# Cross-entropy on one core: compute pipelined over the chunk borders of the last 16384 columns, and the first prediction load on SyncE's queue

## The chip, the cores and the metric

One core of a Trainium2 chip. Its engines go by short names: PE (TensorE), DVE (VectorE), ACT (ScalarE), POOL (GpSimd) and SyncE (SP), which here only issues DMAs and waits. SBUF is the memory in which the kernel's tiles lie. In the table of DMA queues POOL's DMAs are called software_dynamic and SyncE's hardware_dynamic (the prediction's HWDGE). The metric is the device time of one execution in microseconds (us), median over runs. Times inside an execution are read from the profile and count from the start of its span. They end about 2 us below the metric.

## The reference

```python
def reference(pred, target):            # both 8192 x 8192 float32
    eps = 1e-7
    pred = np.clip(pred, eps, 1 - eps)
    return -(target * np.log(pred) + (1 - target) * np.log(1 - pred))
```

`target` is 0 or 1, so the kernel computes -ln|p + t - 1|. Two arrays are read and one is written, 268 MB each.

## The kernel before

The arrays are seen as 128 partitions x 524288 columns. Two rings in SBUF hold 32768 columns each, predictions in float32 (overwritten by the result) and targets in bfloat16 (the DMA casts: the page counts 671.10 MB on POOL's queue, which is the targets at two bytes each, where 536.87 MB are read and 268.44 MB written). The columns go through in 38 chunks: small ones at the start, thirty of 16384, small ones at the end. Every DMA is issued by POOL. A load waits for the store that frees its place in the ring (POOL did so 30 times, 1084.9 us in all).

```python
def chunk_widths(total):
    head = [4096, 4096, 8192]
    tail = [8192, 4096, 2048, 1024, 1024]
    big = 16384
    ...
def load(k):
    c, w = at(k), widths[k]
    nc.gpsimd.dma_start(out=ring_t[:, c : c + w], in_=dram(target_f, cols[k], w))
    nc.gpsimd.dma_start(out=ring_p[:, c : c + w], in_=dram(pred_f, cols[k], w))

def store(k):
    c, w = at(k), widths[k]
    nc.gpsimd.dma_start(out=dram(out_f, cols[k], w), in_=ring_p[:, c : c + w])
# [cut: front(c, w): DVE clip, DVE add of t - 1, ACT Abs, ACT Ln; back(c, w): DVE times -1]
def compute(k):                      # pieces of SUB = 2048 columns
    c, w = at(k), widths[k]
    n = max(1, w // SUB)
    s = w // n
    for i in range(n):
        front(c + i * s, s)
        if i:
            back(c + (i - 1) * s, s)
    back(c + (n - 1) * s, s)         # the chunk is flushed before the next one starts
# [cut: loop over the chunks: store what is done and in the way, load what fits, compute(k)]
```

## Time and profile before

| | before |
|---|---|
| median time, us | 1870.94 (3 runs, 1870.53 to 1871.3) |
| span of the profiled run, us | 1868.8 |
| DMA engines busy | 99.9% |
| DVE, ACT busy | 63%, 52% |

The kernel lives at the rate of its DMA engines (busy 99.9% of the span). Hold on to 16416: these are the packets of POOL's queue. Divided by 16 engines it is 1026, and 1026 is 114 DMAs times 9: in the trace 1824 of the packets have 4 bytes, so each engine has eight packets of data and one of 4 bytes for each DMA.

The end, in stretches; the last two columns are the mean busy share of the 16 DMA engines and GB/s.

```profile
core 0: us, DVE busy (x) ACT busy (x) POOL busy (x), PEclk, DMA share, GB/s
1842.00:1850.00 8.00, 4.66 (x3) 3.21 (x3) 0.96 (x1) 1.00 0.95 412
1850.00:1857.00 7.00, 3.64 (x4) 3.20 (x3) 0.53 (x1) 1.00 0.97 417
1857.00:1861.00 4.00, 1.94 (x3) 1.97 (x2) 0.53 (x1) 1.00 0.57 237
1861.00:1865.00 4.00, 0.69 (x1) 0.15 (x1) 0.25 (x1) 1.00 0.09 38
1865.00:1868.00 3.00, 0.00 (x0) 0.00 (x0) 0.29 (x1) 1.00 0.43 175
```

And POOL's issues of the last four stores, from the timeline (start, duration, and in brackets the idle time before and what ended it).

```profile
1844.03 0.96 POOL L79 DMA_DIRECT2D out_dram<-ring_p  x1 [11.39 <-DVE ring_p L94]
1852.64 0.53 POOL L79 DMA_DIRECT2D out_dram<-ring_p  x1 [7.65 <-DVE ring_p L94]
1857.40 0.53 POOL L79 DMA_DIRECT2D out_dram<-ring_p  x1 [4.23 <-DVE ring_p L94]
1864.75 0.54 POOL L79 DMA_DIRECT2D out_dram<-ring_p  x1 [6.82 <-issue]
```

From 1857 us on the DMA engines run out of work (share 0.57, then 0.09). A share of 0.06 is one engine of 16. The last store carries a mark: its wait ended in "issue", that is, in nothing that the profile shows. DVE's last negation ended at 1861.87 us. The other three went out 0.3 us after their negations, this one 2.88 us after.

One more reading, used all through. A DMA's completion semaphore is counted up sixteen times (1824 counts for 114 DMAs, as many as there are packets of 4 bytes), which is read here as once by each of the 16 DMA engines, and the trace has the times. The sixteenth count is the landing; the distance from a middle count to the last is the lag of the slowest engine. For the store of the last 16384-column chunk but one, the first count came at 1782.19, a middle one at 1782.73, the last at 1788.55 us: the slowest engine is 5.8 us behind.

### The profile page before, as it was taken

To read this page: it belongs to the slowest core of one execution; us is meant where nothing else is said; L and a number is where in the kernel's file an instruction comes from. 1 tells how busy PE (TensorE), PEld (TensorE's weight loads), DVE (VectorE), ACT (ScalarE), POOL (GpSimd) and SP (SyncE) were. 2 spreads that over 40 slices of the span, in tenths; PEclk is the share of its full clock that TensorE was granted. 3 is DMA by queue.
4 is the path that set the end of the run, shared out by engine and by line. 5 is a ranking of instruction groups with operands and counts; after the bars stand their busy time and mean duration, and the time that the engine had idled before them with its cause. 6 is when DMAs were issued, how large, how long until landed. Compare 5 with 4: busy or idle time off the path is not lost.

```text
span 1868.8 us, 1563 instructions
## 1 busy us (share of the span) xinstructions
DVE 1178.6 (63%) x772; ACT 976.3 (52%) x516; POOL 65.4 (3%) x118
## 2 busy tenths in 40 slices
DVE  4557755577555775557755577555776556755595
ACT  3446544565444654446544466444664446644474
POOL 1000000000000000000000000000000000000010
DMA  9999999999999999999999999999999999999998
GB/s 292 359 358 338 348 400 371 337 355 342 393 386 339 341 352 387 384 351 339 345 386 389 351 344 337 383 395 344 352 344 365 400 358 339 354 355 395 374 335 349
DMA packets 16427, 671.19 MB, mean 359 GB/s; under 512 B 1824, under 2 KB 1824, under 8 KB 2720
## 3 DMA queue, kind: packets, MB, share of 16 engines
q0 software_dynamic: 16416, 671.10, 99.9%
q14 instruction: 11, 0.09, 0.0%
HBM read 536.87 MB, written 268.44 MB: 431 GB/s over the span
## 4 chain that ended last, share of the span: by engine, by line
DMA 34%; issue 30%; DVE 27%; ACT 7%; POOL 1%; another core or an unknown queue 1%; POOLq 0%; PEldq 0%
DMA ring_p<-in_pred_dram 32%; DVE ring_p L86 13%; DVE ring_p L94 7%; DVE ring_p L83 7%; ACT ring_p L89 3%; ACT ring_p L90 3%; DMA out_dram<-ring_p 2%; POOL out_dram L79 1%; POOL ring_t L74 1%; POOL ring_p L75 0%; POOLq L151 0%; POOLq L79 0%; PEldq L151 0%
## 5 line engine op out<-in xcount | busy, mean ns | idle before, releaser
L89 ACT ACTIVATE ring_p<-ring_p 128x2048 f32<-128x2048 f32 (+1 forms) x257 | 488.9, 1902 | 876.0 <-DVE ring_p L86 876.0
L83 DVE TENSOR_SCALAR ring_p<-ring_p 128x2048 f32<-128x2048 f32 (+1 forms) x257 | 312.9, 1218 | 552.9 <-DMA ring_p<-in_pred_dram 552.9
L86 DVE SCALAR_TENSOR_TENSOR ring_p<-ring_t,ring_p 128x2048 f32<-128x2048 bf16 (+1 forms) x257 | 586.9, 2284 | 8.8
L90 ACT ACTIVATE ring_p<-ring_p 128x2048 f32<-128x2048 f32 (+1 forms) x257 | 489.2, 1903 | 8.1
L94 DVE TENSOR_SCALAR ring_p<-ring_p 128x2048 f32<-128x2048 f32 (+1 forms) x257 | 313.1, 1218 | 120.8 <-ACT ring_p L90 120.8
L75 POOL DMA_DIRECT2D ring_p<-in_pred_dram x38 | 21.9, 576 | 1094.1 <-DMA out_dram<-ring_p 1084.9
L79 POOL DMA_DIRECT2D out_dram<-ring_p x38 | 22.1, 581 | 700.3 <-DVE ring_p L94 689.9
L74 POOL DMA_DIRECT2D ring_t<-in_target_dram x38 | 21.8, 574 | 5.3 <-DMA ring_t<-in_target_dram 4.4
L62 ACT ACT_TABLE_LOAD x1 | 1.3, 1283 | 0.7 <-PEq L140 0.7
L61 DVE MEMSET warm<- 1x8 f32 x1 | 0.1, 65 | 0.8 <-PEq L140 0.8
L62 ACT ACTIVATE warm<-warm 1x8 f32<-1x8 f32 x1 | 0.2, 207 | 0.0
L140 POOL MEMSET const-float32-0.0<- 128x1 f32 x1 | 0.1, 98 | 0.2 <-issue 0.2
L140 POOL MEMSET const-bfloat16-1.0<- 128x1 bf16 x1 | 0.1, 101 | 0.0
L140 POOL MEMSET const-float32-1.0<- 128x1 f32 x1 | 0.1, 98 | 0.0
L140 POOL MEMSET const-uint8-127<- 128x1 uint8 x1 | 0.1, 98 | 0.0
## 6 DMA issues: line engine op xcount, KB each, us to landing
ring_t<-in_target_dram POOLq DMA_DIRECT2D x30, 4096.0 KB, 55.6
ring_p<-in_pred_dram POOLq DMA_DIRECT2D x2, 4096.0 KB, 29.1
out_dram<-ring_p POOLq DMA_DIRECT2D x2, 4096.0 KB, 30.7
ring_p<-in_pred_dram POOLq DMA_DIRECT2D x3, 2048.0 KB, 20.9
out_dram<-ring_p POOLq DMA_DIRECT2D x3, 2048.0 KB, 53.1
ring_t<-in_target_dram POOLq DMA_DIRECT2D x2, 2048.0 KB, 37.9
ring_t<-in_target_dram POOLq DMA_DIRECT2D x3, 1024.0 KB, 16.5
ring_p<-in_pred_dram POOLq DMA_DIRECT2D x1, 1024.0 KB, 30.7
```

The source lines that it names most:

```text
L61: nc.vector.memset(warm, 1.0)
L62: nc.scalar.activation(out=warm, in_=warm, func=Act.Ln)
L74: nc.gpsimd.dma_start(out=ring_t[:, c : c + w], in_=dram(target_f, cols[k], w))
L75: nc.gpsimd.dma_start(out=ring_p[:, c : c + w], in_=dram(pred_f, cols[k], w))
L79: nc.gpsimd.dma_start(out=dram(out_f, cols[k], w), in_=ring_p[:, c : c + w])
L83: nc.vector.tensor_scalar(out=p, in0=p, scalar1=EPS, scalar2=1 - EPS, op0=Alu.max, op1=Alu.min)
L86: nc.vector.scalar_tensor_tensor(out=p, in0=t, scalar=1.0, in1=p, op0=Alu.subtract, op1=Alu.add)
L89: nc.scalar.activation(out=p, in_=p, func=Act.Abs)
L90: nc.scalar.activation(out=p, in_=p, func=Act.Ln)
L94: nc.vector.tensor_scalar(out=p, in0=p, scalar1=-1.0, scalar2=None, op0=Alu.mult)
L140: nc = _bacc.Bacc("TRN2", target_bir_lowering=False, num_devices=1)
```

## The change

The intent: no flush between the last five chunks, so that DVE need not wait for ACT at each border and the last stores go out sooner; and an earlier first byte by loading the first predictions from SyncE while POOL is still issuing the first target load.

```diff
-        nc.gpsimd.dma_start(out=ring_p[:, c : c + w], in_=dram(pred_f, cols[k], w))
+        queue = nc.sync if k == 0 else nc.gpsimd
+        queue.dma_start(out=ring_p[:, c : c + w], in_=dram(pred_f, cols[k], w))
 # [cut]
+        for k, c, w, last in pieces:          # pieces of all chunks in one list
+            front(c, w)
+            waiting.append((k, c, w, last))
+            if len(waiting) > LAG:            # LAG = 1
+                finish_one()                  # back() of the oldest; at a chunk's last piece store it, load what fits
+
+            if last and cols[k] + widths[k] <= total - RING // 2:
+                while waiting:                # all chunks but the last five: full flush, as before
+                    finish_one()
```

Nothing is added to the work of DVE, ACT or the DMA engines (by the two pages DVE is busy 1178.6 and 1178.3 us, ACT 976.3 in both, and 671.19 MB are moved in both). POOL's sequence of DMAs stays as it was but for the first prediction load, and DVE's order differs only in the last five chunks.

More of the change, by code (lines that the diff above doesn't have):

```diff
@@ L14 @@
 SUB = 2048
+LAG = 1
 def chunk_widths(total):
@@ L60 @@
     warm = pool.tile([1, 8], fp32, name="warm", tag="warm")
-    nc.vector.memset(warm, 1.0)
-    nc.scalar.activation(out=warm, in_=warm, func=Act.Ln)
     widths = chunk_widths(total)
@@ L70, in at, with load_t, load_p @@
         return c
-    def load(k):
+    def load_t(k):
         c, w = at(k), widths[k]
         nc.gpsimd.dma_start(out=ring_t[:, c : c + w], in_=dram(target_f, cols[k], w))
-        nc.gpsimd.dma_start(out=ring_p[:, c : c + w], in_=dram(pred_f, cols[k], w))
+    def load_p(k):
+        c, w = at(k), widths[k]
+        queue = nc.sync if k == 0 else nc.gpsimd
+        queue.dma_start(out=ring_p[:, c : c + w], in_=dram(pred_f, cols[k], w))
     def store(k):
@@ L96, in back, with load_what_fits, finish_one @@
         )
-    def compute(k):
-        c, w = at(k), widths[k]
+    pieces = []
+    for k, w in enumerate(widths):
         n = max(1, w // SUB)
-        s = w // n
         for i in range(n):
-            front(c + i * s, s)
-            if i:
-                back(c + (i - 1) * s, s)
-        back(c + (n - 1) * s, s)
-    with tc.manual_schedule():
-        stored = loaded = 0
-        for k in range(len(widths)):
-            while loaded < len(widths):
-                end = cols[loaded] + widths[loaded]
-                while stored < k and end > cols[stored] + RING:
-                    store(stored)
-                    stored += 1
-                if end > cols[stored] + RING:
-                    break
-                load(loaded)
-                loaded += 1
-            compute(k)
-        while stored < len(widths):
-            store(stored)
-            stored += 1
+            pieces.append((k, at(k) + i * (w // n), w // n, i == n - 1))
+    stored = 0
+    loaded = 0
+    def load_what_fits():
+        nonlocal loaded
+        while (
+            loaded < len(widths)
+            and cols[loaded] + widths[loaded] <= (cols + [total])[stored] + RING
+        ):
+            load_t(loaded)
+            load_p(loaded)
+            loaded += 1
+    with tc.manual_schedule():
+        load_what_fits()
+        nc.vector.memset(warm, 1.0)
+        nc.scalar.activation(out=warm, in_=warm, func=Act.Ln)
+        waiting = []
+        def finish_one():
+            nonlocal stored
+            k, c, w, last = waiting.pop(0)
+            back(c, w)
+            if last:
+                store(k)
+                stored = k + 1
+                load_what_fits()
+        for k, c, w, last in pieces:
[6 more added lines that the diff above has]
+                    finish_one()
+        while waiting:
+            finish_one()
 _INS = ['pred', 'target']
```

## The prediction

> **What bounds the kernel now.** The DMA engines: the page's DMA strip shows 9 in all slices but the last, its queue table 99.9% of 16 engines' span; DVE is busy 63%, ACT 52% (busy table). In the trace, 16384-column transfers land 19.3 us apart (1762.9, 1782.2: first of a transfer's sixteen completion counts). 8.39 MB in 19.3 us is 435 GB/s[...]. 96 such transfers are about 1851 us of the 1868.8 us span. The other 18 us: the start, a slow engine, the end.
>
> The sixteen counts show one lagging engine: from about 700 us on its count comes 4 to 6 us after the median (1788.55 against 1782.7). It sets the end, not compute: the last five stores but one land there at 1846.9, 1856.5, 1861.4, 1863.9, 1865.1 us, gaps equal to their bytes, without idle, while the other engines run dry from 1857 us (DMA share 0.47, then 0.06, in fine windows). Only the last 512 KB store, issued at 1864.75, adds a hole: it lands at 1867.66, 2.6 us after its predecessor in place of 1.2.
>
> **What the change does.** By the instruction order, POOL's DMA sequence is the same but for the first prediction load, DVE's differs only in the last five chunks, ACT's not at all. No byte or vector operation is added or removed; the 30 middle chunks stay.
>
> - Head: POOL issues its first DMA at 1.27 us; first packets start at 2.6 us and are slow for 1 us. SyncE is free at about 0.7 us. [...] no HWDGE transfer is in this trace. Estimate: data flows 0.7 us earlier (0.3 to 1.3), all passed on, as the queue never runs dry afterwards. That chunk 0's loads now interleave is off the critical path: the first store waits behind 33 MB of loads anyway.
> - Tail, compute: borders between the last chunks cost DVE waits on ACT of 2.2 to 3.9 us. From 1809.5 us, with steady pieces of 4.6 us and 1024-wide ones of 2.5 us, stores are issued at about 1832 (unchanged), 1841 (before 1844), 1845 (1852.6), 1848 (1857.4), 1850 (1864.75). Compute ends 12 us earlier.
> - Tail, DMA: almost all of this is off the critical path. The slow engine has queued work until 1865.1 in any case; the last store now follows at once and lands 1.2 us later, 1866.3 in place of 1867.66: gain 1.3 us.
>
> Sum: 1870.94 - 0.7 - 1.3 = 1868.9 us. Range 1866.7 to 1870.6. Chances: faster by over 2% 0.005, within 2% 0.99, slower 0.005.
>
> **What would show it.** First DMA packets at about 2 us; middle landings earlier by the same 0.3 to 1.3 us; the last DVE negation at about 1849 us in place of 1861.2; all stores issued before 1851 us; from 1857 us only a small DMA share (0.06 is one engine) for 7 to 9 us with POOL done; the lagging engine's stores 4.9, 2.5, 1.2, 1.2 us apart.
>
> **What would make it wrong.** The lag grew in jumps of 0.5 to 1 us; 1 to 2 us more or less of it moves the time as much. If SyncE's descriptors start no sooner, or interleaving slows both queues, the head gains nothing. If the last store was held by something other than DVE (done at 1861.9), earlier stores may be held too, though with queued work that costs nothing.

The sum came to 1868.9 us: 1870.94 less 0.7 for the head and 1.3 for the last store. The head's 0.7 us was an estimate: about 0.57 us of it is in the trace before (POOL's first issue at 1.27 us, SyncE free at about 0.7), the rest is not shown. The 1.3 us stand on the landings given in the text.

## More of the kernel before

The experiments ran in four rounds, each on another chip and each with its own runs of the kernel before (medians 1870.35 to 1870.88 us): the ratio is taken within a round, and times of different rounds are compared only roughly.

From the page: the DMA strip (busy tenths of the 16 DMA engines in 40 slices) and the table of DMA queues.

```profile
span 1868.8 us, 1563 instructions
...
DVE 1178.6 (63%) x772; ACT 976.3 (52%) x516; POOL 65.4 (3%) x118
...
DMA  9999999999999999999999999999999999999998
...
q0 software_dynamic: 16416, 671.10, 99.9%
q14 instruction: 11, 0.09, 0.0%
```

## The result, and the profile after

| | before | after |
|---|---|---|
| median time, us | 1871.07 (4 runs, 1870.53 to 1871.3) | 1873.76 (4 runs, 1871.99 to 1874.89) |
| span of the profiled run, us | 1868.8 | 1873.0 |
| first DMA packet, us | 2.64 | 1.74 |
| last store issued, us | 1864.75 | 1850.94 |
| last landing, us | 1867.66 | 1867.65 |
| from there to the end of the span, us | 1.1 | 5.4 |

The ratio of the fast runs is 1.0014, 95% interval 0.9997 to 1.0031. Ratios here are the mean time of one kernel's fast runs over that of the other's of the same rounds, so not quite the ratio of the medians. By the 2% rule the two are the same. But the prediction was 1868.9 us with 1870.6 as its upper end, and no run of the change came below 1871.99.

The same parts of the page after. POOL now has 113 DMAs: 16272 / 16 = 1017 = 113 x 9.

```profile
span 1873.0 us, 1564 instructions
...
DVE 1178.3 (63%) x772; ACT 976.3 (52%) x516; POOL 64.2 (3%) x117
...
DMA  9999999999999999999999999999999999999997
...
q0 software_dynamic: 16272, 669.00, 99.4%
q1 hardware_dynamic: 144, 2.10, 0.3%
q14 instruction: 11, 0.09, 0.0%
```

The end in stretches, after.

```profile
core 0: us, DVE busy (x) ACT busy (x) POOL busy (x), PEclk, DMA share, GB/s
1842.00:1850.00 8.00, 5.40 (x7) 6.70 (x6) 1.60 (x3) 1.00 1.00 430
1850.00:1857.00 7.00, 0.64 (x1) 0.00 (x0) 0.53 (x1) 1.00 0.94 401
1857.00:1861.00 4.00, 0.00 (x0) 0.00 (x0) 0.00 (x0) 1.00 0.89 371
1861.00:1865.00 4.00, 0.00 (x0) 0.00 (x0) 0.00 (x0) 1.00 0.21 89
1865.00:1868.00 3.00, 0.00 (x0) 0.00 (x0) 0.00 (x0) 1.00 0.06 23
1868.00:1870.00 2.00, 0.00 (x0) 0.00 (x0) 0.00 (x0) 1.00 0.00 0
1870.00:1873.00 3.00, 0.00 (x0) 0.00 (x0) 0.00 (x0) 1.00 0.00 0
```

POOL's last four stores, after.

```profile
1842.16 0.53 POOL L84 DMA_DIRECT2D out_dram<-ring_p  x1 [8.24 <-DVE ring_p L99]
1846.17 0.53 POOL L84 DMA_DIRECT2D out_dram<-ring_p  x1 [3.48 <-DVE ring_p L99]
1848.63 0.53 POOL L84 DMA_DIRECT2D out_dram<-ring_p  x1 [1.93 <-DVE ring_p L99]
1850.94 0.53 POOL L84 DMA_DIRECT2D out_dram<-ring_p  x1 [1.77 <-DVE ring_p L99]
```

The tail did what was intended: compute is over by 1851 us, the DMA engines stay busy until about 1860.5 us, then a few late ones go on, and at the end the slowest alone (share 0.06). But in the last two stretches nothing runs at all, no engine and no DMA, for 5 us, and the program has not ended. What is it waiting for? The table of waits, for SyncE's queue, before:

```profile
SPq L151 <- DMA out_dram<-ring_p: 1866.9, 3, 1846.2
SPq L151 <- PEq L151: 0.8, 2, 0.4
```

and after:

```profile
SPq L175 <- DMA out_dram<-ring_p: 1866.4, 5, 1856.7
SPq L175 <- PEq L175: 5.2, 2, 4.7
```

The columns are total, times, longest. SyncE stands at the closing barrier for 4.7 us in place of 0.4. The table puts the wait down to PE's sequencer. The records of the sequencers, which the page does not count as busy time, say more: PE, ACT, DVE and SyncE are all released within 0.05 us, by POOL, and POOL does so 0.1 us after its closing DRAIN, an instruction that the kernel's author did not write.

```
POOL        DRAIN starts   takes   ends      last landing   ends after it
before         1864.73      3.30   1868.03     1867.66         0.37
after          1850.92     21.39   1872.30     1867.65         4.66
```

So two questions are open. Why does the drain end so late? And why did the last landing not come 2 us earlier, as predicted?

### The profile page after: what moved, and what is told of

Its sections match the earlier page's. It is cut to its first block, busy times and chain, and to the rows that moved or that the text cites. A ratio compares the mean times of both kernels' runs of the same rounds, so it can differ in the third digit from the quotient of the medians.

```text
span 1873.0 us, 1564 instructions
## 1 busy us (share of the span) xinstructions
DVE 1178.3 (63%) x772; ACT 976.3 (52%) x516; POOL 64.2 (3%) x117
## 2 busy tenths in 40 slices
DMA packets 16427, 671.19 MB, mean 358 GB/s; under 512 B 1824, under 2 KB 1824, under 8 KB 2720
## 3 DMA queue, kind: packets, MB, share of 16 engines
q0 software_dynamic: 16272, 669.00, 99.4%
## 4 chain that ended last, share of the span: by engine, by line
DMA 36%; issue 27%; DVE 27%; ACT 7%; POOL 1%; another core or an unknown queue 1%; POOLq 0%; PEldq 0%
DMA ring_p<-in_pred_dram 32%; DVE ring_p L91 13%; DVE ring_p L99 7%; DVE ring_p L88 7%; DMA out_dram<-ring_p 4%; ACT ring_p L94 3%; ACT ring_p L95 3%; POOL out_dram L84 1%; POOL ring_t L75 0%; POOL ring_p L80 0%; POOLq L175 0%; POOLq L84 0%; PEldq L175 0%
```

## The experiments

Thirteen runs were made (one of them the change again), and all gave the right result. "Descriptors" below is a count for each of the 16 DMA engines: of each POOL DMA the rows that fall to one engine, and one for the completion. One DMA over 128 partitions counts 9, which agrees with the packets of the kernel before, eight of data and one of 4 bytes. The expectations speak of descriptors written; no trace shows the writing. For the padding loads of 4-byte rows, which come below, the packets do not show the count either (see `e6_plus_2`): the times bear it out.

### First four: early entry into the drain, or the second queue?

Theory D: the drain overruns because it is entered long before the last landing. Rival S: the SyncE queue is at fault.

Only the head part, on the kernel before (`e1_head_only`):

```diff
-        nc.gpsimd.dma_start(out=ring_p[:, c : c + w], in_=dram(pred_f, cols[k], w))
+        queue = nc.sync if k == 0 else nc.gpsimd
+        queue.dma_start(out=ring_p[:, c : c + w], in_=dram(pred_f, cols[k], w))
```

> The kernel before with only the first prediction load moved to SyncE. Theory D (POOL's closing drain overruns when it is entered long before the last store has landed): this kernel issues its last store late, as before, so the drain is short (about 3 us) and ends within 0.6 us of the last landing; the head gain of 0.9 us is kept: about 1870.1 us (1869.5 to 1870.7). Rival S (the second, SyncE queue costs something at the end or makes one DMA engine lag more): 1872 to 1875 us, as in the change.

Measured: 1874.08 us against 1870.41 before, ratio 1.0022 (1.0008 to 1.0036). The last landing was early (1865.78 us), but the drain, entered at 1861.59, ended at 1871.43. This speaks for S.

Only the tail part (`e2_tail_only`):

```diff
-        queue = nc.sync if k == 0 else nc.gpsimd
+        queue = nc.gpsimd
```

> The change with the first prediction load put back on POOL's queue, so only the order of compute and stores in the last chunks changes. Theory D: the drain starts near 1851 us and ends 1 to 5 us after the last landing, times scattered over 1871.5 to 1876 us. Rival S: no overrun, tail gain of 1.3 us kept, about 1869.6 us with little scatter (0.8 us as before).

Measured: 1869.68 us, ratio 0.9996 (0.9983 to 1.0008). The drain was entered at 1853.49, 13.5 us before the last landing, and ended 0.37 us after it. D has fallen: early entry costs nothing here. S had forecast 1869.6 us, and came near it for the wrong reason, as `e7_before_111` will show. SyncE's wait at the barrier was short again:

```profile
SPq L175 <- PEq L175: 0.8, 2, 0.4
```

Beside it, an unasked find: the last store again went out 2.88 us after the last negation (1850.63, 1853.51), the very delay seen before.

The change, with POOL waiting for the last landing by semaphore (`e3_pool_waits`):

```diff
         while waiting:
             finish_one()
+        c_end = at(len(widths) - 1)
+        nc.gpsimd.memset(ring_p[0:1, c_end : c_end + 1], 0.0)
```

> The change, and after the last store POOL writes one element of the last piece, so that it waits for that store by its semaphore and enters its closing drain only when everything has landed (that element was stored already, the result stays right). Theory D: drain under 0.6 us, the time falls to 1868.5 to 1870.6 us (below 1869 if the lagging DMA engine is as before, near 1870.5 if it lags as in the change's profile), scatter under 1 us. Rival S: still 1872 to 1875 us, since both queues are as in the change.

Measured: 1877.47 us, ratio 1.0038 (1.0026 to 1.0051), worse than either theory had it. Everything had landed at 1866.26, the drain was entered at 1866.30, and it still took 9.41 us. So the drain takes time with nothing left to land, and about twice the 4.66 us by which it ended after the last landing in the change. SyncE's line in the waits of this kernel:

```profile
SPq L178 <- PEq L178: 9.8, 2, 9.4
```

The change, with the stores of the last 16384 columns on SyncE (`e4_tail_on_sp`):

```diff
-        nc.gpsimd.dma_start(out=dram(out_f, cols[k], w), in_=ring_p[:, c : c + w])
+        queue = nc.sync if cols[k] >= total - RING // 2 else nc.gpsimd
+        queue.dma_start(out=dram(out_f, cols[k], w), in_=ring_p[:, c : c + w])
```

> The change with the stores of the last 16384 columns issued by SyncE, so POOL's last DMA is the store issued near 1813 us, which lands near 1848 us. Theory D: POOL's drain ends by about 1855 us, hidden; SyncE waits by semaphore; 1868.3 to 1870.6 us, little scatter. Rival S: more traffic on the SyncE queue, so no better than the change, 1872 to 1876 us.

Measured: 1868.5 us, ratio 0.9988 (0.9975 to 1.0). There are six times as many packets on the SyncE queue as in the change, and no loss at the end, against S as written. (D's forecast for this run was met, but D had fallen with the two runs before.) POOL's drain was over at 1855.96, 4.45 us after POOL's own last landing at 1851.51, out of everybody's way.

### Next four: the count of POOL's descriptors

The kernels with a short drain had 1026 descriptors, those with a long one 1017 or 972. And in both kernels with 1026 one store, POOL's 114th DMA, came 2.88 us after its negation with no cause shown. If the count decides, the boundary lies between 1017 and 1026 by these runs. Theory N, not shown so far: the drain is long below the boundary and short past it, and the DMA that crosses it is held.

The change plus one load of 128 rows x 4 bytes on POOL, which nothing reads (`e5_plus_9`):

```diff
+    pad0 = pool.tile([128, 1], fp32, name="pad0", tag="pad0")
         load_what_fits()
+        nc.gpsimd.dma_start(out=pad0, in_=pred[0:128, 0:1])
```

> The change plus one 512-byte load on POOL's queue that nothing reads, so POOL issues 114 DMAs again, as before, with 9 descriptors for each of the 16 engines (8 rows and a completion): 114 x 9 = 1026. Theory N (POOL's overrun depends on how many descriptors it has written[...]): a stall of about 2.9 us appears before POOL's 114th DMA (the last store), hidden behind queued stores, the drain ends within 0.5 us of the last landing, and the time is 1868 to 1870 us. Rival S (the SyncE queue itself makes the drain overrun): unchanged, drain 4 to 6 us after the last landing, 1872 to 1875 us.

Measured: 1868.61 us against 1870.35 before, ratio 0.9989 (0.9974 to 1.0004). An added, useless load took about 4 us off the change (`e6_plus_2`, next, has the comparison within one round: 1872.42 us). The stall before the last store appeared (negation ends 1849.38, store 1852.26), and the drain ended 0.37 us after the last landing. Here the last two stores:

```profile
1847.38 0.53 POOL L85 DMA_DIRECT2D out_dram<-ring_p  x1 [1.94 <-DVE ring_p L100]
1852.26 0.54 POOL L85 DMA_DIRECT2D out_dram<-ring_p  x1 [4.35 <-issue]
```

The same with 16 rows in place of 128 (`e6_plus_2`):

```diff
+    pad0 = pool.tile([16, 1], fp32, name="pad0", tag="pad0")
         load_what_fits()
+        nc.gpsimd.dma_start(out=pad0, in_=pred[0:16, 0:1])
```

> As the run before, but the added load has 16 rows of 4 bytes, so 1 row and a completion for each engine: 114 DMAs, but 113 x 9 + 2 = 1019 descriptors. Theory N by descriptors: [...] no stall before the 114th DMA, and the drain overruns by 4 to 6 us, 1872 to 1875 us. N by number of DMAs: as the run before, 1868 to 1870 us. Rival S: 1872 to 1875 us, told from N by the run before.

Measured: 1872.42 us, ratio 1.0012 (0.9997 to 1.0027). The drain ended 4.70 us after the last landing, and there was no stall before the 114th DMA:

```profile
1846.56 0.53 POOL L85 DMA_DIRECT2D out_dram<-ring_p  x1 [1.94 <-DVE ring_p L100]
1848.86 0.53 POOL L85 DMA_DIRECT2D out_dram<-ring_p  x1 [1.77 <-DVE ring_p L100]
```

This pair is the cleanest. Both have 114 DMAs on POOL, and both have 16304 packets in the queue table (32 more than in the change, so two for each engine: the eight 4-byte rows of one engine show as one packet), but one counts 1026 descriptors and the other 1019. The number of DMAs, of packets, and the SyncE queue are all the same in the two; the count of descriptors is not. The two differ also by 112 four-byte rows of data, 448 bytes. And they narrow the boundary by measurement alone: it lies between 1019 (drain 4.70 us after the last landing) and 1026 (0.37 us).

The kernel before with nothing on SyncE and fewer DMAs (`e7_before_111`):

```diff
-    head = [4096, 4096, 8192]
+    head = [8192, 8192]
```

> The kernel before with its first two chunks of 4096 columns joined to one of 8192: 111 DMAs on POOL, 999 descriptors an engine, nothing on SyncE. Theory N: no stall before the last store (it goes out 0.3 us after the last negation, gaining about 1.2 us), but the drain overruns by 4 to 6 us after the last landing: 1872 to 1877 us. Rival S: drain within 0.5 us of the last landing, 1869 to 1871 us.

Measured: 1874.85 us, ratio 1.0023 (1.0008 to 1.0038). The drain ended 5.47 us after the last landing with no DMA on SyncE's queue at all:

```profile
SPq L151 <- PEq L151: 5.9, 2, 5.5
```

S has fallen: the overrun needs no SyncE queue, which in the change had only taken one DMA away from POOL.

The kernel before with three padding loads (`e8_before_117`):

```diff
+            if k == 3:      # pad0, pad1, pad2: [128, 1] each
+                nc.gpsimd.dma_start(out=pad0, in_=pred[0:128, 0:1])   # and pad1, pad2 likewise
             compute(k)
```

> The kernel before plus three 512-byte loads on POOL's queue: 117 DMAs, 1053 descriptors an engine, nothing on SyncE. Theory N: the 2.9 us stall moves to the 114th DMA, now the third store from the end (4096 columns) and no longer the last; the drain ends within 0.5 us of the last landing; the last store is issued 0.3 us after the last negation; about 1870 to 1871.5 us. Rival S: stall stays before the last store; same time as before.

Measured: 1869.62 us, ratio 0.9997 (0.998 to 1.0013). The stall moved to the 114th DMA, now the fourth store from the end (117 - 114 = 3 follow it; the expectation miscounted it as the third), while the width, 4096 columns, was as expected. The last store goes out right after its negation:

```profile
1846.98 0.54 POOL L82 DMA_DIRECT2D out_dram<-ring_p  x1 [13.97 <-issue]
1853.02 0.53 POOL L82 DMA_DIRECT2D out_dram<-ring_p  x1 [5.50 <-DVE ring_p L97]
1857.77 0.53 POOL L82 DMA_DIRECT2D out_dram<-ring_p  x1 [4.22 <-DVE ring_p L97]
1862.53 0.53 POOL L82 DMA_DIRECT2D out_dram<-ring_p  x1 [4.23 <-DVE ring_p L97]
```

So the "issue" mark of the kernel before went with the 114th DMA, which takes the count to 1026; the 114th of `e6_plus_2`, which takes it to 1019, was not held.

### The lagging engine, the change again, and the head alone

All prediction loads and stores on SyncE, only the casting target loads on POOL (`e9_two_queues`):

```diff
-        queue = nc.sync if k == 0 else nc.gpsimd
+        queue = nc.sync
 # and in store(k):
-        nc.gpsimd.dma_start(out=dram(out_f, cols[k], w), in_=ring_p[:, c : c + w])
+        nc.sync.dma_start(out=dram(out_f, cols[k], w), in_=ring_p[:, c : c + w])
```

> The change with all prediction loads and all stores on SyncE; POOL keeps only the target loads, which cast. POOL's last DMA is issued near 1790 us, so its closing drain is over long before the end. If the lagging DMA engine (5 to 7 us behind at the end) owes its lag to POOL's descriptors, two thirds of which are gone, the lag shrinks to 2 us or less and the time falls to 1863 to 1866 us; if not, it stays near 5 us and the time is 1867.5 to 1869 us as with only the last stores moved; if mixing two queues in the steady state disturbs the order of loads and stores, slower than 1871 us.

Measured: 1953.73 us, ratio 1.0451. The time is that of the third case of the expectation; that a disturbed order is the cause is not shown. By the page the DMA engines were busy 98.3% of 1949.4 us, against 99.9% of 1868.8 us before: of the 81 us lost, about 31 are idle time and about 49 are packets that took longer for the same bytes. SyncE's prediction loads waited for stores to land for 1466.6 us in total, in 30 waits (1084.9 us for POOL in the kernel before), but this proves nothing: in `e12_684` below the same wait came to 1775.6 us and the DMA engines stayed busy 99.8%. The lag was gone (0.6 us at the end), but in about 33 us of idle time a late engine may catch up, so this run does not tell whether POOL's descriptors cause the lag.

The change once more (`e10_after_again`, no edit):

> The change once more, unaltered, for a second profile and its scatter. If its first profile's lag of 6.8 us was chance, the last landing comes near 1865.7 us (the other kernels with early last stores: 1865.0 to 1867.0) and the drain still ends 4.4 to 5 us after it: times 1871.5 to 1875 us. If the change itself makes the engine lag more: last landing near 1867.6 us again.

Measured: 1872.51 us (1872.26 to 1873.39), ratio 1.0009 (0.9997 to 1.0022). The last landing came at 1865.84 and the drain ended 4.66 us after it. The lag at the end was 5.85 us, in the first profile of the change 6.8 us, in that of the kernel before 5.8 us. The middle count of the store of the last 16384-column chunk came at 1840.52 us, in the first profile of the change at 1841.37, in the kernel before at 1841.10. So the late landing of the first profile did not come again; about half of it was lag and half came from all engines being later. Two profiles do not tell whether that was chance or the chip.

Only the head, with one padding load to bring POOL back to 1026 (`e11_head_plus_9`; the edits of `e1_head_only` and one padding load at k == 3):

> Only the first prediction load on SyncE, and one 512-byte load added on POOL so that it again writes 1026 descriptors an engine. Against 1874.1 us without the added load: theory N gives a 2.9 us stall before the last store, a short drain, and the head gain alone: 1869.3 to 1870.2 us, 0.4 to 1 us under the kernel before. Rival S: 1873 to 1876 us.

Measured: 1870.09 us against 1870.88, ratio 0.9996 (0.9983 to 1.0008). Against `e1_head_only` (1874.08, in another round) one padding load gives back 4 us. What is left under the kernel before, 0.8 us, is the head gain, inside the noise of the ratio.

### A law for the drain, and a test of it

The thirteen traces up to here fit this: let p be 4.57 ns, the fitted figure, times the descriptors. Up to 1019, the drain takes p once after it is entered (and the last DMA's 0.53 us are out), and p once more after POOL's last landing. From 1026 on it ends 0.37 us after that landing, and 4.57 ns later for each descriptor past 1026 (0.49 us with 1053). For `e7_before_111`: p = 999 x 4.57 ns = 4.57 us; 1861.25 + 0.53 + 4.57 = 1866.35, which is later than the last landing at 1865.46; plus 4.57 is 1870.92. The trace has 1870.93. For `e3_pool_waits`, entered with everything landed: 1866.30 + 0.09 (its memset) + 2 x 4.65 = 1875.69; the trace has 1875.71. Four more, `e2_tail_only`, `e5_plus_9`, `e10_after_again` and `e11_head_plus_9`, which the table below leaves out, fit within 0.02 us. Because a fit can flatter itself, two counts not seen so far were predicted, one look each.

All prediction loads on SyncE, stores and target loads on POOL (`e12_684`):

```diff
-        queue = nc.sync if k == 0 else nc.gpsimd
+        queue = nc.sync
```

> The change with all prediction loads on SyncE, target loads and stores on POOL: 76 DMAs on POOL, 684 descriptors an engine; the last store is POOL's. Its time is expected to be worse (the order of loads and stores is disturbed) and is not the point. Fit: the drain ends 684 x 4.57 ns = 3.1 us after the last landing (2.9 to 3.4). Rival, two fixed values: 4.4 to 4.8 us, as in all runs that ended between 972 and 1019.

Measured: 3.14 us.

```profile
SPq L175 <- PEq L175: 3.0, 2, 2.6
```

The time was 1873.61 us against 1870.82 before, one run each: 2.8 us more, which is the longer drain (3.14 in place of 0.37 us). The loss from a disturbed order that was expected did not come. The lag at the end was 7.1 us, though POOL had a third fewer descriptors than in the change.

Twenty padding loads (`e13_1197`):

```diff
                 store(k)
+                if 3 <= k < 23:      # pad: [128, 32]
+                    nc.gpsimd.dma_start(out=pad[:, k : k + 1], in_=pred[0:128, k : k + 1])
```

> The change plus twenty 512-byte loads on POOL's queue, one after each of twenty stores: 133 DMAs, 1197 descriptors an engine[...]. Fit: the drain ends 0.37 us plus 171 x 4.57 ns = 1.15 us after the last landing (1.0 to 1.35), and the 2.6 us stall sits at the 114th DMA in mid-kernel, harmless. Rival, two fixed values: 0.37 to 0.5 us, as with 1026 and 1053.

Measured: 1.15 us (time 1869.39 us against 1870.82, one run each); and POOL's 114th DMA, a store in mid-kernel, went out at 1695.92 us, 2.86 us after its negation had signalled at 1693.06:

```profile
1695.92 0.55 POOL L85 DMA_DIRECT2D out_dram<-ring_p  x1 [23.08 <-issue]
```

Both counts fell on the fit, far from the rival's fixed values.

| run | descriptors | drain entered | POOL's last landing | drain ends after it | fit |
|---|---|---|---|---|---|
| `e9_two_queues` | 342 | 1829.79 | 1889.59 | 1.59 | 1.56 |
| `e12_684` | 684 | 1855.06 | 1867.92 | 3.14 | 3.13 |
| `e4_tail_on_sp` | 972 | 1811.89 | 1851.51 | 4.45 | 4.44 |
| `e7_before_111` | 999 | 1861.25 | 1865.46 | 5.47 | 5.45 |
| after | 1017 | 1850.92 | 1867.65 | 4.66 | 4.65 |
| `e1_head_only` | 1017 | 1861.59 | 1865.78 | 5.65 | 5.63 |
| `e6_plus_2` | 1019 | 1848.84 | 1864.96 | 4.70 | 4.66 |
| before | 1026 | 1864.73 | 1867.66 | 0.37 | 0.37 |
| `e8_before_117` | 1053 | 1862.51 | 1866.80 | 0.49 | 0.49 |
| `e13_1197` | 1197 | 1849.64 | 1865.74 | 1.15 | 1.15 |

The law is a fit to these times; no record shows what POOL does in them. The 0.37 us with 1026 descriptors and the 2.6 us of the stall at the crossing (2.88 in place of 0.3 us after the negation, 2.86 in `e13_1197`; six kernels have it) are measured sizes without an explanation.

The best versions found are `e4_tail_on_sp` (1868.5 us) and `e5_plus_9` (1868.61 us), both about 0.1% under the kernel before, at the edge of what the intervals resolve. For use the first is the better: it needs no padding and does not depend on a count.

## Why the prediction was wrong

The forecast was 1870.94 - 0.7 - 1.3 = 1868.9 us; 1873.76 us came out.

- **What bounds the kernel.** Right. 435 GB/s in the steady state (8.39 MB in 19.3 us), and a lagging engine, 5.8 us behind in the kernel before, that set the last landing in the change (1867.65 us). It is the slowest of several late ones, not the only one.
- **Head, 0.7 us.** Right at the start; its full passing on is not shown. The first packet came 0.9 us earlier (1.74, 2.64), and at 62 us landings were still 0.8 us earlier (61.72, 62.47), though POOL's own first packet came later (5.53 in place of 2.64). Near 1841 us the middle count was 0.3 us later in the first profile of the change and 0.6 us earlier in the second. `e11_head_plus_9` shows 0.8 us in the time, inside its noise. From SyncE's issue at 0.74 us to the first packet it took 1.0 us, on POOL's path 1.4 us (1.27, 2.64).
- **Tail, compute.** Right. Stores at 1833.0, 1842.2, 1846.2, 1848.6 and 1850.9 us, each about 1 us later than forecast.
- **Tail, DMA, 1.3 us.** The mechanism was right: the hole before the last store closed. The lagging engine's stores landed 4.9, 2.5, 1.2 and 1.2 us apart (1857.85, 1862.71, 1865.16, 1866.41, 1867.65). The last landing, forecast by these two gains at 1865.7 us, came at 1867.65 in the first profile, whose slowest engine lagged 1 us more and whose other engines were about 1 us later than forecast, and at 1865.84 in the second. The risk of the lag was named. One sign did not come: from 1857 us the DMA share was to be small, and it was 0.89 until 1861, with all stores issued before 1851 us. The two gains together, with the drain short again, are `e5_plus_9`: 1.7 us by the medians, of the 2.0 forecast.
- **The step that failed: the sum ended at the last landing.** There was no term for the program's end. It took for granted, without saying so, that the 0.4 us between the last landing and the end of POOL's drain would stay. It did see that POOL's sequence was "the same but for the first prediction load", and that one load was the matter: it took POOL from 1026 descriptors to 1017, so the boundary between 1019 and 1026 was no longer crossed, and the drain that had ended 0.37 us after the last landing ended 4.66 us after it. With this term the sum is 1868.9 + 4.3 = 1873.2 us, between the two medians measured for the change, 1873.76 and 1872.51.
- **What could have been seen.** The prediction asked whether the last store had been held by something other than DVE (2.9 us by its numbers), and set this aside as costing nothing where work is queued. With work queued it cost nothing (`e5_plus_9`); in the kernel before it made the hole of 1.3 us that the prediction counted as the tail's gain. It was the trace of the same boundary: all six kernels with this stall had a short drain (0.37 to 1.15 us).

Taken apart, the parts have these signs, of which only the second is clear of the noise (an interval reaches about 2.5 us either way): tail alone -0.7 us by the medians (1869.68, 1870.41), head alone +3.7 us (1874.08, 1870.41), head with the count mended -0.8 us (1870.09, 1870.88). The expected gain was made, as far as these runs resolve it, and was given back at the end with interest.

What stays open: why some DMA engines lag, the slowest by 4.9 to 7.5 us after a middle count near the end, in all runs but `e9_two_queues`, and by a different amount from run to run. The lag set the last landing where the last stores were issued early; in the kernel before, the last store went out so late that all sixteen counts came within 0.2 us.

## What to carry to other kernels

A kernel need not end with its last landing (the change ended 5.4 us after it): put the closing barrier into the sum, and look in the waits who comes to it last, above all when a change moves or removes a DMA (one load moved cost 3.7 us in `e1_head_only`). When POOL issues DMAs, keep its last one well ahead of the end (here: last stores from SyncE), so that its drain is hidden (over at 1855.96 us in a span of 1865.8). And an idle time that ends in "issue" just where the profile shows no cause (here 2.6 us) is worth a question before it is called free.
